# First attention head's keys, values and queries loaded after named gate tiles of the input projection

## Chip, cores and metric

One core of a Trainium2 (trn2) chip. The metric is the device time of one execution in microseconds. Times shown as a median come from three runs of the kernel; the rows come from one profiled execution of it.

## What is computed

Two layers of an encoder over 2048 tokens of width 1024. Each layer projects its normed input to 4128 columns, gives them to three branches, gates each branch with SiLU, and projects back. Cut to what matters here:

```python
h = rms_norm(x, norm_pre[layer])
proj = h @ w_in[layer]                       # 2048 x 4128
(gq, gk, gv, gg, gaf, gab, dq, dk, dv, dg, hq, hzf, hzb, hi, hg) = jnp.split(proj, offs, axis=-1)
y_a = gla_branch(...)                        # gated linear attention, a scan over chunks
y_b = diff_branch(dq, dk, dv, dg, ...)       # softmax attention, below
y_c = hgrn_branch(...)                       # gated linear recurrence, a scan over chunks
y = jnp.concatenate([y_a, y_b, y_c], axis=-1) @ w_out[layer]
x = x + rms_norm(y, norm_post[layer])

# diff_branch: 4 heads, two queries and two keys of 64 each, values of 128
q, k = rope(q, pos) * (DIFF_HD ** -0.5), rope(k, pos)
s = jnp.einsum('cbhqd,cbhkd->cbhqk', qblk, k)          # c = 0, 1
p = softmax(s);  w = p[0] - lam * p[1];  o = w @ v
o = rms_norm(o, norm_w) * (1.0 - lambda_init)
y_b = merge_heads(o) * jax.nn.silu(dg)
```

## The kernel before

**Projection.** Each fp32 matrix product is made of three: the operands are split into a high and a low part, and high by high, high by low and low by high are added in PSUM. The columns of a layer's input projection are taken in 18 blocks, mostly of 256 columns (the lists `first` and `rest`, lines 487 to 508). All 18 run for tokens 0 to 1023 (part 0) and then again for tokens 1024 to 2047 (part 1); in part 1 the split weights of a block come back from DRAM in two loads of 1 MB, whi and wlo, which POOL issues at line 226. Between the blocks of part 1 the two scans are recorded (`scans`), up to block 13. From block 14 (SC_END) on, what is left is: the second query block (`do_qk`, index 14, in which queries get their rotation), and three gate blocks (`do_gate`): 15 and 16 for attention's gate columns, 17 for the recurrence's. The pool `ak` with attention's keys (ks), values (vt) and queries (aqh, aql, the high and the low part) is opened at SC_END.

**A query tile** (`do_qk`, lines 366 to 378): 2 x 24 matmuls (L330); DVE multiplies out of PSUM into ru (L369) and rz (L371); POOL L372 adds; ACT L374 rounds to rh; POOL L375 takes the rest; SP stores rh and ru to dr_q (L377, L378), 256 KB each.

**A gate tile** (`do_gate`, 256 tokens x 256 columns, 4 tiles in a block and part): 48 matmuls (`mm_time`, L339); DVE L428 copies PSUM to z; ACT L350, L351, L352 make the softplus part lse; DVE L354 makes lsm, the log of the sigmoid; ACT L430 takes its exponential in place; POOL L432 multiplies z by the norm weights nw; POOL L433 multiplies by lsm; SP L434 stores 256 KB to dr_gate.

nw has one buffer. It is loaded by SP at L412 at the head of each block: two loads of 64 KB for blocks 15 and 16, which DVE L414 then scales, and four of 32 KB for block 17. All of ru, rz, rh, z, lse and lsm share one tag of six buffers, so a tile can't go on while the operation or store that frees its buffer has not happened.

**Attention's first operands.** `load_q(0, 0..2)` at SC_END: 3 x 8 loads of 64 KB on SP. `head_keys(0)` at SC_END + 1: four loads of 512 KB, issued by POOL for head 0 and by SP for the others. `head_values(0)` at SC_END + 2: one load of 1 MB issued by POOL. Attention's scores (L928, L929) read ks and aqh, aql; DVE L933 takes the maximum; ACT L942 the exponential. Head 1's keys have the second buffer of ks and are loaded during the gate blocks too.

**What sets the order.** The kernel is written against a tile framework that follows data dependences, inserts the semaphores, and sets each engine's order with a planner of its own before it runs. An engine executes its instructions in that order. A DMA's issue stands in the order of the engine that issues it and waits there for what it needs, so that what stands behind it waits too. A load into a tile that nobody else uses waits for the tile's memory alone.

Of the kernel before, what the change touches and what calls it, by code (L numbers as in the profile page):

```python
# [61 lines left out]
def tile_hybrid_encoder(  # L62
# [9 lines left out]
    nc = tc.nc  # L72
# [49 lines left out]
    def psum_close(key):  # L122
        psum.pop(key)[0].close()
# [168 lines left out]
    for l in range(DEPTH):  # L292
# [15 lines left out]
        with ExitStack() as s1:  # L308
# [7 lines left out]
            def acc(shape, name, part):  # L316
                turn[0] += 1
                return one_bank(shape, name, "m" if part == 0 and turn[0] % 2 else "s")

            def wload(c0, n, part, halves=False, scale=1.0):  # L320
                return w_again(wp, c0, n) if part else wload_into(wp, l, c0, n, halves, scale)
# [13 lines left out]
            def mm_rows(ps, w, t, n):  # L335
                g, cnt = t // 4, 0
                for k in range(KC):
                    for a, b in ((0, hhi), (0, hlo), (1, hhi)):
                        nc.tensor.matmul(ps, b[g][:, t % 4, k], w[a][:, k, :n], start=cnt == 0, stop=cnt == 3 * KC - 1)  # L339
                        cnt += 1  # L340

            def mm_time(w, t2, one_pool=False):
                ps = acc([P, 2, 256], "pp", 1 if one_pool else t2 // 4)
                for j in range(2):
                    mm_rows(ps[:, j], w, 2 * t2 + j, 256)
                return ps

            def log_sig(z, keep=None):
                e = ev.tile([P, 512], F32, tag="t", name="lse")
                nc.scalar.activation(e, z, AF.Abs)  # L350
                nc.scalar.activation(e, e, AF.Exp, scale=-1.0)  # L351
                nc.scalar.activation(e, e, AF.Ln, bias=one_t)  # L352
                m = ev.tile([P, 512], F32, tag="t", name="lsm")
                nc.vector.scalar_tensor_tensor(m, z, 0.0, e, op0=ALU.min, op1=ALU.subtract)  # L354
                return e, m
# [24 lines left out]
            def t2_rows(ap, t2):  # L380
                return ap[256 * t2:256 * t2 + 256, :].rearrange("(j p) c -> p j c", p=P)
# [19 lines left out]
                        nc.sync.dma_start(dr_vr[t0:t0 + 1024, i].rearrange("(c p) n -> c p n", p=P),  # L401
                                          bass.AP(odd.tensor, odd.offset + (P - 1) * 512, [(P * 512, 8), (-512, P), (1, 64)]))

            low = {}

            def do_gate(c0, d0, part):
                w = wload(c0, 288 if d0 == 0 else 256, part)
                nw = ev.tile([P, 256], F32, tag="nw", name="nw", bufs=1)
                src = {0: gla_norm, 768: hgrn_norm}.get(d0, diff_norm)
                n = src.shape[-1]  # L410
                for i in range(0, 256, n):
                    nc.sync.dma_start(nw[:, i:i + n], src[l:l + 1].to_broadcast([P, n]))  # L412
                if src is diff_norm:
                    nc.vector.tensor_scalar(nw, nw, 1.0 - lam_init, None, op0=ALU.mult)  # L414
                for t2 in range(4 * part, 4 * part + 4):
                    z = ev.tile([P, 512], F32, tag="t", name="z")
                    if d0 == 0:
                        if t2 % 2 == 0:
                            low[t2 // 2] = ev.tile([P, 4, 32], F32, tag="low", name="low", bufs=2)
                        for j in range(2):  # L420
                            t = 2 * t2 + j
                            ps = acc([P, 288], "pp", part)
                            mm_rows(ps, w, t, 288)
                            nc.vector.tensor_copy(z[:, 256 * j:256 * j + 256], ps[:, :256])
                            nc.scalar.copy(low[t2 // 2][:, t % 4], ps[:, 256:])
                    else:
                        ps = mm_time(w, t2)
                        nc.vector.tensor_copy(z, ps.rearrange("p j c -> p (j c)"))  # L428
                    _, m = log_sig(z)
                    nc.scalar.activation(m, m, AF.Exp)  # L430
                    zn = z.rearrange("p (j c) -> p j c", j=2)
                    nc.gpsimd.tensor_tensor(zn, zn, nw.unsqueeze(1).to_broadcast([P, 2, 256]), op=ALU.mult)  # L432
                    nc.gpsimd.tensor_tensor(z, z, m, op=ALU.mult)  # L433
                    nc.sync.dma_start(t2_rows(dr_gate, t2)[:, :, d0:d0 + 256], zn)  # L434

            def do_ch(c0, dst, scale, part):
                w = wload(c0, 256, part)
# [309 lines left out]

            kv, qs_of, ga_of = {}, {}, [None]

            def head_keys(h):  # L750
                k = ak.tile([P, 2, L], F32R, tag="ks", name="ks", bufs=2)
                r = slice(64 * (h % 2), 64 * (h % 2) + 64)
                for p0 in range(0, P, 32):
                    (nc.sync if h else nc.gpsimd).dma_start(
                        k[p0:p0 + 32].bitcast(F32), dr_k[h // 2, p0 // 64, p0 // 32 % 2, r].rearrange("(c p) t -> p c t", p=32))
                ks = [k[:, 0], k[:, 1]]
                kv[h] = [ks, None]

            def head_values(h):
                v = ak.tile([P, NT, P], F32, tag="vt", name="vt", bufs=2)  # L760
                nc.gpsimd.dma_start(v, dr_v[:, h * P:(h + 1) * P].rearrange("(c p) n -> p c n", p=P))
                kv[h][1] = v

# [4 lines left out]
            def load_q(h, qp):  # L768
                qh = ak.tile([P, 2, 256], F32R, tag="aqh", name="aqh", bufs=3)
                ql = ak.tile([P, 2, 256], F32R, tag="aql", name="aql", bufs=3)  # L770
                r = slice(64 * (h % 2), 64 * (h % 2) + 64)
                for i, q in enumerate((qh, ql)):
                    for p0 in range(0, P, 32):
                        nc.sync.dma_start(q[p0:p0 + 32].bitcast(F32), dr_q[h // 2, p0 // 64, i, r, qp * 256:(qp + 1) * 256]
                                          .rearrange("(c p) t -> p c t", p=32))
                qs_of[h, qp] = qh, ql
# [8 lines left out]
            for i, b in enumerate(first + rest):  # L785
                b(1)
                scans(LAG * SCHED[i] if i < SC_END else len(work))
                if i == SC_END:
                    sc_st.close()
                    psum_close("m")  # L790
                    psum_open("t", f"pst{l}", "right")
                    at_st = ExitStack()
                    ak = at_st.enter_context(tc.tile_pool(name=f"ak{l}", bufs=1, side="left"))
                    for qp in range(3):
                        load_q(0, qp)
                if i == SC_END + 1:
                    head_keys(0)
                if i == SC_END + 2:
                    head_values(0)
            w_in_st.close()  # L800
            psum_close("s")
            psum_open("b", f"psb{l}", "left")
# [387 lines left out]
```

## Time and profile before

| | |
|---|---|
| median of 3 runs | 3580.6 us (3577.68 to 3582.16) |
| the profiled execution | 3580.0 us, its span 3578.0 us |
| mean granted clock of TensorE | 0.988 of full speed |
| TensorE (PE) busy | 3491.2 us, 98% |
| TensorE's weight loads (PEld) | 3151.1 us, 88% |
| VectorE (DVE) | 2331.3 us, 65% |
| ScalarE (ACT) | 2046.3 us, 57% |
| GpSimd (POOL) | 1280.7 us, 36% |
| DMA | 544.59 MB, mean 152 GB/s |

Shares are of the span. All times in rows are microseconds from the span's start. A row of an engine's timeline ends, in brackets, with how long the engine was idle ahead of the instruction and what ended that. SPq is SP's DMA queue; a DMA in the chain of waits counts from its issue to its landing. The granted clock is given as a share of full speed: 1.00 is 2.4 GHz, 0.50 is 1.2 GHz.

### The profile page before, as it was taken

How to read it: one execution, taken by the hardware profiler on the slowest of the kernel's cores; microseconds unless marked ns; L12 is line 12 of the kernel's file. 1: busy time of each engine (PE TensorE's matmuls, PEld its weight loads, DVE VectorE, ACT ScalarE, POOL GpSimd, SP SyncE). 2: the span in 40 equal slices, each digit the busy share in tenths (PEclk: the TensorE clock that was granted, in tenths of full speed). 3: DMA queues.
4: the chain of work that ended last, by engine and by line, in shares of the span. 5: the costliest groups of instructions: out<-in, count | busy, mean ns of one | idle time of the engine just before them, and what ended most of it. 6: DMA issues, size and time to landing. Idle time of an engine off the chain costs nothing.

```text
span 3578.0 us, 62684 instructions
## 1 busy us (share of the span) xinstructions
PE 3491.2 (98%) x23296; PEld 3151.1 (88%) x23296; DVE 2331.3 (65%) x4164; ACT 2046.3 (57%) x4692; POOL 1280.7 (36%) x1302
## 2 busy tenths in 40 slices
PE   7999999999899999999999999999998999999999
PEld 7898988988889999998898999889888889999887
DVE  5333578775299988985324336777843998989733
ACT  4531457653378888874226225576524888888722
POOL 4237310013466655610032472000134765656100
PEclk9999999999999999999999999999999999999999
DMA  6667545545653353214356665555465423433143
GB/s 238 214 230 241 202 151 172 164 145 179 184 140 75 108 137 100 89 50 156 121 205 232 221 228 180 172 163 167 134 190 167 129 73 116 132 93 101 35 135 118
DMA packets 323120, 544.59 MB, mean 152 GB/s; under 512 B 49088, under 2 KB 208512, under 8 KB 304128
## 3 DMA queue, kind: packets, MB, share of 16 engines
q1 hardware_dynamic: 300032, 426.54, 37.8%
q0 software_dynamic: 20672, 111.94, 9.8%
q8 instruction: 185, 3.03, 0.4%
q10 hardware_dynamic: 2112, 2.10, 0.2%
q14 instruction: 119, 0.97, 0.1%
HBM read 313.83 MB, written 228.59 MB: 152 GB/s over the span
## 4 chain that ended last, share of the span: by engine, by line
PE 75%; DVE 13%; DMA 5%; ACT 4%; issue 1%; SPq 1%; POOL 0%; DVEq 0%; ACTq 0%; POOLq 0%
PE pp L339 15%; PE pp L330 15%; PE po L991 10%; PE pob L1100 9%; PE s L928 5%; PE s L929 5%; PE pt L980 5%; DVE mx L933 4%; PE pm L619 2%; DVE e L974 2%; PE po L692 2%; PE pu L714 1%; PE poi L875 1%; DMA dr_q<-rh 1%; DMA gt<-dr_gg 1%
## 5 line engine op out<-in xcount | busy, mean ns | idle before, releaser
L933 DVE TENSOR_REDUCE mx<-s 128x1 f32<-128x1024 f32 x512 | 623.2, 1218 | 59.5 <-PE s L929 58.0
L339 PE MATMUL pp<-whi,hhi 128*128 128x256 f32 (+1 forms) x2048 | 591.5, 289 | 19.9 <-issue 14.2
L942 ACT ACTIVATE e<-s,mx 128x1024 f32<-128x1024 f32 x512 | 572.7, 1123 | 30.1 <-DVE mx L933 12.0
L339 PE MATMUL pp<-wlo,hhi 128*128 128x256 f32 (+1 forms) x2048 | 588.9, 288 | 0.0
L339 PE MATMUL pp<-whi,hlo 128*128 128x256 f32 (+1 forms) x2048 | 587.7, 287 | 0.4 <-DVE hlo L198 0.4
L991 PEld LDWEIGHTS po<-vt,wt 128*128 128x128 f32 x4096 | 534.3, 191 | 46.0 <-ACT o L998 3.5
L991 PE MATMUL po<-vt,wt 128*128 128x128 f32 x4096 | 540.1, 275 | 1.6 <-ACT o L998 1.6
L928 PE MATMUL s<-ks,aqh 128*128 128x512 f32 x1024 | 449.8, 439 | 12.9 <-ACT e L942 11.2
L339 PEld LDWEIGHTS pp<-whi,hhi 128*128 128x128 f32 x2048 | 393.8, 192 | 23.1 <-issue 21.7
L330 PE MATMUL pp<-hhi,whi 128*128 128x512 f32 x1024 | 407.7, 398 | 0.0
L330 PE MATMUL pp<-hlo,whi 128*128 128x512 f32 x1024 | 406.7, 397 | 0.0
L330 PE MATMUL pp<-hhi,wlo 128*128 128x512 f32 x1024 | 404.5, 395 | 0.0
L929 PE MATMUL s<-ks,aql 128*128 128x512 f32 x1024 | 403.4, 394 | 0.0
L339 PEld LDWEIGHTS pp<-whi,hlo 128*128 128x128 f32 x2048 | 394.2, 193 | 1.8 <-DVE hlo L198 0.8
L339 PEld LDWEIGHTS pp<-wlo,hhi 128*128 128x128 f32 x2048 | 393.4, 192 | 1.6 <-issue 0.2
L984 ACT COPY wt<-pt 128x512 f32<-128x512 f32 x512 | 301.3, 588 | 152.3 <-PE pt L980 149.2
L974 DVE SCALAR_TENSOR_TENSOR e<-e,gam 128x1024 f32<-128x1024 f32 x256 | 350.0, 1368 | 0.0
L980 PE MATMUL pt<-ident,e 128*128 128x128 f32 x2048 | 307.8, 273 | 0.4 <-ACT wt L984 0.3
L226 POOL DMA_DIRECT2D whi<-dr_w x32 | 17.6, 550 | 667.5 <-PE pp L339 341.7
L980 PEld LDWEIGHTS pt<-ident,e 128*128 128x128 f32 x2048 | 239.9, 141 | 1.8 <-ACT wt L984 1.0
L928 PEld LDWEIGHTS s<-ks,aqh 128*128 128x128 f32 x1024 | 194.9, 190 | 42.5 <-ACT e L942 18.2
L330 PEld LDWEIGHTS pp<-hhi,whi 128*128 128x128 f32 x1024 | 192.7, 188 | 43.5 <-issue 0.2
(184 smaller groups left out, 6846.2 us busy)
## 6 DMA issues: line engine op xcount, KB each, us to landing
dr_w<-whi SPq DMA_DIRECT2D x30, 1024.0 KB, 3.9
dr_w<-wlo SPq DMA_DIRECT2D x30, 1024.0 KB, 4.9
whi<-dr_w POOLq DMA_DIRECT2D x30, 1024.0 KB, 5.5
wlo<-dr_w POOLq DMA_DIRECT2D x30, 1024.0 KB, 8.6
wraw<-in_w_in_dram POOLq DMA_DIRECT2D x56, 512.0 KB, 6.3
dr_gate<-z SPq DMA_DIRECT2D x64, 256.0 KB, 2.4
aqh<-dr_q SPq DMA_DIRECT2D x256, 64.0 KB, 2.1
aql<-dr_q SPq DMA_DIRECT2D x256, 64.0 KB, 2.1
```

The costliest lines, as they stand in the source:

```text
L330: nc.tensor.matmul(ps.rearrange("p (a t) -> p a t", t=P), w[a][:, k, c:c + P], b[g][:, :, k], start=n == 0, stop=n == 3 * KC - 1)
L339: nc.tensor.matmul(ps, b[g][:, t % 4, k], w[a][:, k, :n], start=cnt == 0, stop=cnt == 3 * KC - 1)
L619: nc.tensor.matmul(pm[hd][:, c], kc[rows, cs], qc[rows, cs], start=True, stop=True)
L928: nc.tensor.matmul(s[:, i], self.qh[:, c, js], kk, start=True, stop=False)
L929: nc.tensor.matmul(s[:, i], self.ql[:, c, js], kk, start=False, stop=True)
L933: nc.vector.tensor_reduce(mx[:, k:k + 1], self.s[k].rearrange("p a n -> p (a n)"), axis=AX.X, op=ALU.max, negate=True)
L942: nc.scalar.activation(self.es[c][:, n * 1024:(n + 1) * 1024], self.s[kk].rearrange("p a n -> p (a n)"), AF.Exp, bias=self.mx[:, m:m + 1], ...
L974: nc.vector.scalar_tensor_tensor(es[0][:, hs], es[1][:, hs], gm[:, 8 + n:9 + n], es[0][:, hs], op0=ALU.mult, op1=ALU.add)
L980: nc.tensor.transpose(pt[:, i], self.es[0][:, (4 * q + i) * P:(4 * q + i + 1) * P], ident)
L984: nc.scalar.copy(wt, self.pt[q])
L991: nc.tensor.matmul(self.po, self.wt[q][:, i], self.v[:, k], start=k == 0, stop=k == NT - 1)
L1100: nc.tensor.matmul(pos[:, n], a[:, k], b[k][:, n * 512:(n + 1) * 512], start=cnt == 0, stop=cnt == 3 * KC - 1)
```

## The change

`do_gate` leaves the last tile's lsm, as it is after L430, in `late[0]`. A new helper, `after_block(t)`, copies one column of it into tile t on DVE, and then the load of t overwrites that column. The load so waits for the copy, and the copy for the exponential of the gate tile recorded last. For head 0 alone, the keys get such a copy (recorded after block 15), the values and the first three pairs of query tiles too (recorded after block 16, to which the query loads are moved from SC_END). These are eight copies in a layer, 16 in all. Nothing else is changed; TensorE's and ACT's orders are the same as before, and from line 435 on line numbers are higher by one, from `head_keys` on by seven to eleven.

```diff
--- before.py
+++ after.py
@@ -401,7 +401,7 @@
                         nc.sync.dma_start(dr_vr[t0:t0 + 1024, i].rearrange("(c p) n -> c p n", p=P),
                                           bass.AP(odd.tensor, odd.offset + (P - 1) * 512, [(P * 512, 8), (-512, P), (1, 64)]))
 
-            low = {}
+            low, late = {}, [None]
 
             def do_gate(c0, d0, part):
                 w = wload(c0, 288 if d0 == 0 else 256, part)
@@ -432,6 +432,7 @@
                     nc.gpsimd.tensor_tensor(zn, zn, nw.unsqueeze(1).to_broadcast([P, 2, 256]), op=ALU.mult)
                     nc.gpsimd.tensor_tensor(z, z, m, op=ALU.mult)
                     nc.sync.dma_start(t2_rows(dr_gate, t2)[:, :, d0:d0 + 256], zn)
+                    late[0] = m
 
             def do_ch(c0, dst, scale, part):
                 w = wload(c0, 256, part)
@@ -747,8 +748,14 @@
 
             kv, qs_of, ga_of = {}, {}, [None]
 
+            def after_block(t):
+
+                nc.vector.tensor_copy(t, late[0][:, :1])
+
             def head_keys(h):
                 k = ak.tile([P, 2, L], F32R, tag="ks", name="ks", bufs=2)
+                if not h:
+                    after_block(k[:, 0, :1])
                 r = slice(64 * (h % 2), 64 * (h % 2) + 64)
                 for p0 in range(0, P, 32):
                     (nc.sync if h else nc.gpsimd).dma_start(
@@ -758,6 +765,8 @@
 
             def head_values(h):
                 v = ak.tile([P, NT, P], F32, tag="vt", name="vt", bufs=2)
+                if not h:
+                    after_block(v[:, 0, :1])
                 nc.gpsimd.dma_start(v, dr_v[:, h * P:(h + 1) * P].rearrange("(c p) n -> p c n", p=P))
                 kv[h][1] = v
 
@@ -770,6 +779,8 @@
                 ql = ak.tile([P, 2, 256], F32R, tag="aql", name="aql", bufs=3)
                 r = slice(64 * (h % 2), 64 * (h % 2) + 64)
                 for i, q in enumerate((qh, ql)):
+                    if not h and qp < 3:
+                        after_block(q[:, 0, :1])
                     for p0 in range(0, P, 32):
                         nc.sync.dma_start(q[p0:p0 + 32].bitcast(F32), dr_q[h // 2, p0 // 64, i, r, qp * 256:(qp + 1) * 256]
                                           .rearrange("(c p) t -> p c t", p=32))
@@ -791,12 +802,12 @@
                     psum_open("t", f"pst{l}", "right")
                     at_st = ExitStack()
                     ak = at_st.enter_context(tc.tile_pool(name=f"ak{l}", bufs=1, side="left"))
-                    for qp in range(3):
-                        load_q(0, qp)
                 if i == SC_END + 1:
                     head_keys(0)
                 if i == SC_END + 2:
                     head_values(0)
+                    for qp in range(3):
+                        load_q(0, qp)
             w_in_st.close()
             psum_close("s")
             psum_open("b", f"psb{l}", "left")
```

SP's order in layer 0 at the second query block. In the kernel before (aqh and aql are the query loads, dr_q the stores of a query tile):

```order
L733 DMA dr_u<-ut 64x3x128
L733 DMA dr_u<-ut 64x4x128
L774 DMA aqh<-dr_q 32x2x256 x4
L774 DMA aql<-dr_q 32x2x256 x3
L377 DMA dr_q<-rh 128x512
L774 DMA aql<-dr_q 32x2x256
L774 DMA aqh<-dr_q 32x2x256 x4
L774 DMA aql<-dr_q 32x2x256 x4
L774 DMA aqh<-dr_q 32x2x256 x3
L378 DMA dr_q<-ru 128x512
```

In the changed kernel, from the same two scan stores on (aga loads a piece of the gate):

```order
L734 DMA dr_u<-ut 64x3x128
L734 DMA dr_u<-ut 64x4x128
L791 DMA aga<-dr_gate 128x2x128 x3
L377 DMA dr_q<-rh 128x512
L378 DMA dr_q<-ru 128x512
L377 DMA dr_q<-rh 128x512
```

The 24 query loads no longer stand between the stores.

SP's order at the gate blocks, layer 0, in the kernel before (the dr_gate stores are those of gate blocks 15 to 17; nw are the norm weights, of block 16 and then of block 17):

```order
L434 DMA dr_gate<-z 128x2x256 x3
L412 DMA nw<-in_diff_norm_dram 128x128 x2
L434 DMA dr_gate<-z 128x2x256 x4
L412 DMA nw<-in_hgrn_norm_dram 128x64 x3
L434 DMA dr_gate<-z 128x2x256
L412 DMA nw<-in_hgrn_norm_dram 128x64
L434 DMA dr_gate<-z 128x2x256 x2
L840 DMA woraw<-in_w_out_dram 128x1024 x2
```

In the changed kernel the part up to block 16's stores (the ks here are head 1's keys):

```order
L434 DMA dr_gate<-z 128x2x256 x3
L761 DMA ks<-dr_k 32x2x2048 x2
L412 DMA nw<-in_diff_norm_dram 128x128 x2
L761 DMA ks<-dr_k 32x2x2048 x2
L434 DMA dr_gate<-z 128x2x256 x4
```

and from there to the norm weights of block 17:

```order
L785 DMA aqh<-dr_q 32x2x256 x4
L785 DMA aql<-dr_q 32x2x256 x3
L434 DMA dr_gate<-z 128x2x256
L785 DMA aql<-dr_q 32x2x256
L785 DMA aqh<-dr_q 32x2x256 x4
L785 DMA aql<-dr_q 32x2x256 x4
L785 DMA aqh<-dr_q 32x2x256 x4
L785 DMA aql<-dr_q 32x2x256 x4
L412 DMA nw<-in_hgrn_norm_dram 128x64 x4
L851 DMA woraw<-in_w_out_dram 128x1024 x2
```

Head 1's keys now stand around block 16's norm weights, and the 24 query loads ahead of block 17's.

POOL's order in layer 0 in the kernel before (whi and wlo are a block's weights, ks and vt head 0's keys and values):

```order
L226 DMA whi<-dr_w 128x2048
L226 DMA wlo<-dr_w 128x2048
L372 TENSOR_TENSOR ru<-ru,rz 128x512
L754 DMA ks<-dr_k 32x2x2048 x4
L761 DMA vt<-dr_v 128x16x128
L375 TENSOR_TENSOR ru<-ru,rh 128x512
L372 TENSOR_TENSOR ru<-ru,rz 128x512
```

In the changed kernel, from the weights of block 17 on:

```order
L226 DMA whi<-dr_w 128x2048
L226 DMA wlo<-dr_w 128x2048
L432 TENSOR_TENSOR z<-z,nw 128x512
L761 DMA ks<-dr_k 32x2x2048 x4
L433 TENSOR_TENSOR z<-z,lsm 128x512
L432 TENSOR_TENSOR z<-z,nw 128x512 x2
L433 TENSOR_TENSOR z<-z,lsm 128x512 x2
L432 TENSOR_TENSOR z<-z,nw 128x512
L433 TENSOR_TENSOR z<-z,lsm 128x512
L432 TENSOR_TENSOR z<-z,nw 128x512
L770 DMA vt<-dr_v 128x16x128
L433 TENSOR_TENSOR z<-z,lsm 128x512
```

Keys and values have moved from the query block to the gate tiles, behind block 17's weights.

DVE's order in the changed kernel, layer 0, around the new copies (L753):

```order
L753 CAST ks<-lsm 128x1
L428 COPY z<-pp 128x512
L354 SCALAR_TENSOR_TENSOR lsm<-z,lse 128x512
L428 COPY z<-pp 128x512
L354 SCALAR_TENSOR_TENSOR lsm<-z,lse 128x512
L414 TENSOR_SCALAR nw<-nw 128x256
L428 COPY z<-pp 128x512
L354 SCALAR_TENSOR_TENSOR lsm<-z,lse 128x512
...
L753 COPY vt<-lsm 128x1
L753 CAST aqh<-lsm 128x1
L753 CAST aql<-lsm 128x1
```

The keys' copy follows L354 of block 15's last tile, the others L354 of block 16's last tile; the scaling of nw (L414) stands between.

## Rows read from the trace of the kernel before

**Rows 1.** Chain of waits, layers 0 and 1: start us, us, engine, what.
```profile
888.39 20.99 DMA dr_q<-rh
...
916.51 8.24 DMA dr_q<-ru
928.35 57.84 PE pp L339 x480
...
990.65 1.20 ACT e L942 x2
...
2665.73 19.74 DMA dr_q<-rh
...
2705.51 59.32 PE pp L339 x480
...
2770.34 1.20 ACT e L942 x2
```

**Rows 2.** TensorE's timeline: start us, us, instruction [idle before <-what ended it].
```profile
912.41 0.55 PE L339 MATMUL pp<-whi,hhi 128*128 128x256 f32 x1 [7.77 <-issue]
...
928.35 0.36 PE L339 MATMUL pp<-whi,hhi 128*128 128x256 f32 x1 [2.07 <-DVE ru L369]
...
2688.51 0.55 PE L339 MATMUL pp<-whi,hhi 128*128 128x256 f32 x1 [6.38 <-issue]
...
2705.51 0.35 PE L339 MATMUL pp<-whi,hhi 128*128 128x256 f32 x1 [3.65 <-DVE ru L369]
```

**Rows 3.** Windows: us, busy PE, PEld, DVE, ACT, POOL; PEclk, DMA share, GB/s.
```profile
885.00:905.00 20.00, 19.64 (x87) 15.95 (x85) 0.69 (x1) 1.24 (x2) 7.49 (x9) 1.00 1.00 262
890.00:895.00 5.00, 5.00 (x24) 4.14 (x23) 0.00 (x0) 0.62 (x1) 2.50 (x2) 1.00 1.03 212
...
910.00:915.00 5.00, 2.58 (x12) 2.62 (x13) 1.63 (x3) 0.62 (x1) 3.88 (x5) 0.50 0.64 175
950.00:980.00 30.00, 30.00 (x252) 30.00 (x251) 9.30 (x14) 18.27 (x28) 16.59 (x14) 1.00 0.20 64
```

**Rows 4.** SP's queue: start us, us for the run of issues, what, count.
```profile
896.03 8.50 SPq L774 DMA_DIRECT2D aqh<-dr_q  x4
...
912.57 0.92 SPq L774 DMA_DIRECT2D aql<-dr_q  x2
...
954.10 0.82 SPq L412 DMA_DIRECT2D nw<-in_diff_norm_dram  x2
...
970.24 1.30 SPq L412 DMA_DIRECT2D nw<-in_hgrn_norm_dram  x3
```

**Rows 5.** POOL's timeline, columns as in rows 2.
```profile
885.29 2.18 POOL L754 DMA_DIRECT2D ks<-dr_k  x4
...
959.10 1.70 POOL L432 TENSOR_TENSOR z<-z,nw 128x512 f32<-128x512 f32 x1 [3.64 <-DVE nw L414]
960.87 1.30 POOL L433 TENSOR_TENSOR z<-z,lsm 128x512 f32<-128x512 f32 x1
...
978.57 1.29 POOL L432 TENSOR_TENSOR z<-z,nw 128x512 f32<-128x512 f32 x1 [6.98 <-DVE lsm L354]
```

**Rows 6.** DVE's timeline, columns as in rows 2.
```profile
909.56 0.69 DVE L371 TENSOR_TENSOR rz<-pp,cs 128x512 f32<-128x512 f32 x1 [20.44 <-DMA dr_q<-rh]
...
949.14 0.68 DVE L428 COPY z<-pp 128x512 f32<-128x512 f32 x1
...
952.01 0.69 DVE L354 SCALAR_TENSOR_TENSOR lsm<-z,lse 128x512 f32<-128x512 f32 x1 [2.19 <-ACT lse L352]
...
958.67 0.29 DVE L414 TENSOR_SCALAR nw<-nw 128x256 f32<-128x256 f32 x1 [1.89 <-DMA nw<-in_diff_norm_dram]
```

**Rows 7.** ACT's timeline, columns as in rows 2.
```profile
952.73 0.63 ACT L430 ACTIVATE lsm<-lsm 128x512 f32<-128x512 f32 x1 [0.76 <-DVE lsm L354]
```

**Rows 8.** The page's DMA issues: queue, count, KB each, median us to landing.
```profile
whi<-dr_w POOLq DMA_DIRECT2D x30, 1024.0 KB, 5.5
...
ks<-dr_k POOLq DMA_DIRECT2D x8, 512.0 KB, 14.2
```


## Prediction

> **What bounds the kernel now.** I read the chain of waits first, in the two stretches that the change touches, which I call L0 and L1 (the last projection blocks of layer 0 and layer 1); then TensorE's timeline there, the windows, and the timelines of SP, POOL, DVE and ACT. TensorE is busy for 98% of the span, so a change counts only by the idle TensorE time that it takes away or makes, and by a lower granted clock.
>
> In both layers the chain leaves TensorE once, at the end of the query blocks, for a store: dr_q<-rh, 20.99 us long in L0 and 19.74 in L1 [rows 1]. The DVE operation that needs its buffer waits 20.44 us for it [rows 6]. TensorE then waits 7.77 and 2.07 us in L0, 6.38 and 3.65 in L1 [rows 2]. I count from T0, the end of the last query matmul: 912.41 − 7.77 = 904.64 in L0 and 2688.51 − 6.38 = 2682.13 in L1.
>
> Why is a 256 KB store so slow? From 885 to 905 the DMA engines are full (share 1.00, 262 GB/s) [rows 3]. POOL had just issued four key loads of 512 KB [rows 5, 8], behind weights of 2 × 1024 KB [rows 8] and ahead of 1024 KB of values. On SP's queue the small query loads stand among the stores, and four of them take 8.50 us of issue where two take 0.92 later [rows 4]. The keys, values and queries wait for nothing but free memory, so they go out all at once, while attention starts 100 us later.
>
> What this costs: 480 gate matmuls in a row take 57.84 us [rows 1], 0.1205 each, so a gate tile of 48 takes 5.78 us, and the 576 of three blocks would take 69.4. They end at 928.35 + 57.84 = 986.19 in L0, T0 + 81.6, and at 2705.51 + 59.32 = 2764.83 in L1, T0 + 82.7. Lost: 12.1 and 13.3 us, part of it in the granted clock, 0.50 (1.2 GHz) in the 5 us behind the gap [rows 3]. The first exponential of attention starts at 990.65 and 2770.34 [rows 1]: **T0 + 86.0 and T0 + 88.2**. What the change is worth is how much earlier than this, after T0, that exponential starts.
>
> **What it removes.** The 24 query loads, 2 MB of keys and 1 MB of values of head 0 leave the stretch before T0, and with them the wait on the store. The store should land near the 8.24 us of its twin [rows 1] or sooner, TensorE does not stop at T0, and the gates end at T0 + 69.4. If nothing took the place of the stall, that would be 25.4 us.
>
> **What it adds, cheap.** Sixteen one-column DVE copies, eight to a layer. No such copy is in the trace; above, a 128x256 operation takes 0.29 us [rows 6], below, nothing. I take 0.2: 1.6 us a layer, beside gate work in which DVE is busy 9.3 of 30 us [rows 3]. Cost 0; uncovered, 1.6 a layer. But the copies stand in order on DVE and wait for L430 of a gate tile, as the next tile's z copy does anyway; and SP and POOL wait at the issues behind them.
>
> **What it adds, dear: the norm weights.** In the new order SP issues the norm weights of gate block 16 (nw, two loads) after the first half of head 1's keys, and at the moment when POOL issues the keys of head 0; and those of block 17 (four loads) after all 24 query loads. POOL's L432 needs nw, and six buffers are shared by all gate tiles, so when POOL stops, DVE, ACT and TensorE stop one after the other. Step by step:
>
> - The keys' copy waits for tile 4 of block 15: T0 + 4 × 5.78 + 0.68 + 2.19 + 0.69 + 0.63 [rows 6, 7] = T0 + 27.3. The four issues take 2.18 [rows 5].
> - Around T0 + 25.4 to 30 these are then asked of the DMA engines: weights 2048 KB, keys 2048 KB, half of head 1's keys 1024 KB, gate stores 256 KB, nw 128 KB: 5504 KB, 5.64 MB. At the 262 GB/s of the earlier crowd [rows 3] that is 21.5 us. So nw lands at **N ≈ T0 + 47**. Bounds: the same loads alone took 4.6 us, issued 954.10 [rows 4] and used 958.67 [rows 6]: T0 + 32.8, which binds nothing (TensorE's own pace then sets the end, as with N = T0 + 39.8). At the lowest rate, 212 GB/s [rows 3], 26.6 us: T0 + 52. I take the middle rate, because it was measured with the same keys and weights in flight.
> - From N: nw's scaling 0.29, POOL 1.70 + 3 × 1.30 [rows 5] (two tiles, since the third's buffer waits for them), DVE 0.69 and 0.68, ACT 2.19, DVE 0.69, ACT 0.63 [rows 6, 7], the copies 0.2 and some hops: the first query load is issued at N + 11.3.
> - 24 query loads and one gate store at 0.46 [rows 4] are 11.5, with 1.5 for the 1 MB of values beside them (an estimate: between 0 and the 6.6 by which four loads at 8.50 exceed four at 0.46): nw of block 17 is issued at N + 24.3.
> - It lands 8.3 later (issued 970.24 [rows 4], used 978.57 [rows 5]): N + 32.6. POOL 3 × 1.30: N + 36.5. DVE, ACT, DVE, ACT for the last tile, 4.9, and a gate store that has to land between: the last gate exponential ends, and the first of attention starts, near N + 43 = **T0 + 90**. ACT's order leaves the gate's exponential ahead of attention's.
>
> L0: 90 − 86.0 = +4.0; L1: 90 − 88.2 = +1.8. Sum **+5.8 us**. From 3580.0 (the profiled execution's time, whose span is 3578.0) it gives 3585.8; the median of the runs is 3580.6, so 3586. Each microsecond of N counts twice; N = T0 + 44 breaks even. Between N = T0 + 44 and 48 the time is 3579 to 3588. TensorE idles ahead of attention's first scores, and behind the 7.77 us gap the granted clock was 0.50 [rows 2, 3]; 5 us at half speed would cost 2.5. The chain there runs through ACT, not TensorE [rows 1], so I take 0, and 0 to 2.5 a layer as bounds.
>
> These loads, issued early, held up a store for 20.99 us [rows 1]. A rule speaks against holding them back all the same: the Trainium skill ("DMA: Bandwidth & Descriptors", Rules for kernel authors) says to issue a DMA early and to wait late; by it the present order would be the faster one. The row disagrees for the stretch before T0; for the stretch after it, no row here can.
>
> **Rivals.**
>
> *The transfers don't queue up, N ≤ T0 + 40 (faster).* One mechanism: the packets of nw share the DMA engines with the big loads from the start, instead of landing after them. For it: two norm loads landed in 4.6 us, and the share between 950 and 980 is only 0.20 [rows 3]. Against it: the query loads at 8.50 for four [rows 4], in the same company. Then TensorE's pace sets the tiles up to the query loads, the first exponential comes at T0 + 82.8 (39.8 + 43), and the sum is −3.2 − 5.4 = −8.6: 3572. Nothing lower follows, since nw of block 17 stands behind 24 query loads in any case; without that it would be T0 + 74, 26 us faster. The Trainium skill ("DMA: Bandwidth & Descriptors", Anatomy of one DMA — SWDGE (gpsimd) path) prices a DMA at about 2.0 us plus bytes over 436 GB/s; by that, as an estimate, 5.64 MB would take 13 us, N about T0 + 38, and this rival's time. The 262 GB/s of the full engines [rows 3] disagrees.
>
> *The norm weights land later, N = T0 + 48 to 52, or the query loads are slowed by the values (slower).* The place is SP's queue at gate block 16, the price 2 us of time for each of N, and it decides from N = T0 + 48 on. For it: small loads among the keys were issued at 2.1 us each, not 0.46 [rows 4]; 212 GB/s in the worst 5 us [rows 3]. Against it: fewer small loads stand in this crowd. N = T0 + 50 gives +6.0 more: 3592; T0 + 52, 3596.
>
> *It doesn't do what it says.* The stall at T0 could stay, if the weights alone slow the stores. Then everything of the after-chain shifts by 7.77 and 6.38: about 3600. Against it: the twin store, issued after the crowd, takes 8.24 us, and behind it 480 matmuls run without a gap [rows 1].
>
> **How the numbers follow.** The difference that a measurement of this kernel can tell from none is about 0.2%, 7.2 us: faster below 3573.4, slower above 3587.8. Chances: forecast, N = T0 + 44 to 48, 0.46 (same); late norm weights 0.36 and unchanged stall 0.04 (slower, 0.40); no queueing 0.14 (faster). The range reaches from the faster rival's 3572, with a microsecond of margin 3571, to N = T0 + 52 and the same, 3597; outside I leave the unchanged stall and the ends of the others.
>
> **What would show it.** Right: no TensorE gap at T0, dr_q stores landing within 8 us, gate matmuls in 69 us or so until POOL stops; L414's wait for nw ending near T0 + 47 in both layers, and POOL's L432 idle 10 us and more before; query loads issued from T0 + 58; POOL waiting again for block 17's nw until N + 33; the first exponential at T0 + 90. Wrong: nw landing within 8 us of its issue (then 3572 or less), a first exponential that follows something else than the last gate tile, a stall at T0, or a loss elsewhere, say in the scans, whose order on SP does not change, or at the first scores, if queries or values come later than I have them.

## The result, and the profile after

The changed kernel takes 3601.95 us in the median of five runs (3595.28 to 3609.07), the kernel before 3580.6; the ratio is 1.0063, with a 95% interval of 1.0043 to 1.0083. It is slower, by 15 to 30 us, where no measurable difference was forecast (3586, range 3571 to 3597). The profiled execution has a span of 3605.4 us, against 3578.0.

I read it as the forecast did: by the time from the last query matmul (T0) to the first exponential of attention. TensorE in the changed kernel; columns as in rows 2:

```profile
917.06 0.28 PE L339 MATMUL pp<-whi,hhi 128*128 128x256 f32 x1
...
986.06 0.28 PE L339 MATMUL pp<-wlo,hhi 128*128 128x256 f32 x1
...
1010.28 0.77 PE L939 MATMUL s<-ks,aqh 128*128 128x512 f32 x1 [18.91 <-DVE z L428]
...
2700.87 0.28 PE L339 MATMUL pp<-whi,hhi 128*128 128x256 f32 x1
```

The gaps of [rows 2] are gone: the first gate matmul follows the last query matmul without idle time, so T0 = 917.06 and 2700.87. The query stores that took 20.99 us [rows 1] now land in 2.1; this is the view of DMA issues for 898 to 926 (queue, count, KB each, median us to landing):

```profile
dr_q<-rh SPq DMA_DIRECT2D x6, 256.0 KB, 2.1
```

But TensorE stands still for 18.91 us at attention's start (23.34 in L1). ACT's timeline has the first exponentials (L953, behind the last gate exponential, L430):

```profile
1014.22 0.63 ACT L430 ACTIVATE lsm<-lsm 128x512 f32<-128x512 f32 x1 [1.95 <-DVE lsm L354]
1014.76 1.09 ACT L953 ACTIVATE e<-s,mx 128x1024 f32<-128x1024 f32 x1
...
2798.89 1.11 ACT L953 ACTIVATE e<-s,mx 128x1024 f32<-128x1024 f32 x1 [0.81 <-PE s L940]
```

That is T0 + 97.7 in L0 and T0 + 98.0 in L1, against 86.0 and 88.2 before [rows 1]: +11.7 and +9.8, **+21.5 us** together. The median moved by 21.4.

Where it is lost: POOL, which issues block 17's weights (L226) and 4 us later the keys, waits twice for norm weights, for block 16's and then for block 17's.

```profile
940.83 0.57 POOL L226 DMA_DIRECT2D whi<-dr_w  x1
...
945.30 2.20 POOL L761 DMA_DIRECT2D ks<-dr_k  x4
...
967.28 2.55 POOL L432 TENSOR_TENSOR z<-z,nw 128x512 f32<-128x512 f32 x2 [18.46 <-DVE nw L414]
...
1003.94 2.48 POOL L432 TENSOR_TENSOR z<-z,nw 128x512 f32<-128x512 f32 x2 [21.87 <-DMA nw<-in_hgrn_norm_dram]
```

DVE gives the first wait's end (the new copy that releases the keys, then L414 in both layers):

```profile
944.66 0.15 DVE L753 CAST ks<-lsm 128x1 fp32r<-128x1 f32 x1 [0.70 <-ACT lsm L430]
...
966.85 0.29 DVE L414 TENSOR_SCALAR nw<-nw 128x256 f32<-128x256 f32 x1 [11.41 <-DMA nw<-in_diff_norm_dram]
...
2750.22 0.29 DVE L414 TENSOR_SCALAR nw<-nw 128x256 f32<-128x256 f32 x1 [10.62 <-DMA nw<-in_diff_norm_dram]
```

SP's queue gives the second: block 16's norm weights go out within 0.1 us of POOL's keys, block 17's behind the query loads:

```profile
945.37 0.83 SPq L412 DMA_DIRECT2D nw<-in_diff_norm_dram  x2
...
979.16 2.31 SPq L785 DMA_DIRECT2D aqh<-dr_q  x4
...
984.37 4.88 SPq L785 DMA_DIRECT2D aqh<-dr_q  x4
...
994.93 1.85 SPq L412 DMA_DIRECT2D nw<-in_hgrn_norm_dram  x4
...
2762.54 1.74 SPq L785 DMA_DIRECT2D aqh<-dr_q  x4
...
2777.89 2.04 SPq L412 DMA_DIRECT2D nw<-in_hgrn_norm_dram  x4
```

The windows of the first wait, columns as in rows 3: the DMA engines are full at 218 GB/s. In the kernel before they were busy for a fifth from 950 to 980 [rows 3], when its norm weights of both blocks were loaded.

```profile
950.00:960.00 10.00, 10.00 (x85) 10.00 (x85) 1.39 (x2) 2.96 (x5) 0.00 (x0) 1.00 1.02 218
960.00:970.00 10.00, 10.00 (x86) 10.00 (x85) 0.89 (x2) 0.00 (x0) 2.72 (x3) 1.00 1.03 218
```

The second wait is another matter. While it lasts the DMA engines empty:

```profile
988.00:996.00 8.00, 2.09 (x4) 1.02 (x4) 1.92 (x2) 1.98 (x3) 0.00 (x0) 0.60 0.50 134
996.00:1002.00 6.00, 0.00 (x0) 0.00 (x0) 0.00 (x0) 0.00 (x0) 0.00 (x0) 0.50 0.08 21
```

So block 17's norm weights are late by their place in SP's order (15.8 us from the first query load to their issue), and then by their own landing, 7.3 us for a load among almost idle DMA engines (6.3 in the kernel before). No burst holds them at that point.

### The profile page after: what moved, and what is told of

Same layout as the page of the kernel before. It is cut to its first block, busy times and chain, and to the rows that moved or that the text cites. A ratio compares the mean times of both kernels' runs of the same rounds, so it can differ in the third digit from the quotient of the medians.

```text
span 3605.4 us, 62709 instructions
## 1 busy us (share of the span) xinstructions
PE 3494.7 (97%) x23296; PEld 3149.6 (87%) x23296; DVE 2332.7 (65%) x4180; ACT 2045.5 (57%) x4692; POOL 1272.2 (35%) x1302
## 5 line engine op out<-in xcount | busy, mean ns | idle before, releaser
L953 ACT ACTIVATE e<-s,mx 128x1024 f32<-128x1024 f32 x512 | 572.1, 1122 | 30.0 <-DVE mx L944 10.8
L226 POOL DMA_DIRECT2D whi<-dr_w x32 | 17.7, 553 | 671.0 <-PE pp L330 346.2
```

Of the source, the lines that this page charges most:

```text
L953: nc.scalar.activation(self.es[c][:, n * 1024:(n + 1) * 1024], self.s[kk].rearrange("p a n -> p (a n)"), AF.Exp, bias=self.mx[:, m:m + 1], ...
```

## Experiments

The first theory (A) was the forecast's: POOL waits for norm weights that land late, behind the keys and then behind the query loads. Its rival (B): the burst of loads holds up everything small, and the norm weights are only what waits first.

All were timed beside runs of the kernel before, whose median there was 3587 us; 0.001 of a ratio is 3.6 us. The table has, for L0 and L1, the first exponential after the last query matmul, from each trace as above; the sum against the kernel before's 174.2; and idle time of TensorE that came later, for the two layers. The last column is measured by itself, without the trace.

| run | L0 | L1 | against before | later gap | ratio (95%) |
|---|---|---|---|---|---|
| before | 86.0 | 88.2 | | | 1 |
| changed kernel | 97.7 | 98.0 | +21.5 | | 1.0063 (1.0043 to 1.0083) |
| the same again (e13) | 97.6 | 99.0 | +22.4 | | 1.0066 (1.0047 to 1.0085) |
| e1, norm weights early | 86.9 | 86.1 | −1.2 | | 0.9995 (0.9978 to 1.0011) |
| e2, block 17's alone | 87.2 | 87.1 | +0.1 | | 1.0013 (0.9996 to 1.0030) |
| e3, block 16's alone | 83.9 | 83.0 | −7.3 | | 0.9978 (0.9966 to 0.9990) |
| e4, before, norm weights early | 101.8 | 99.7 | +27.3 | | 1.0079 (1.0057 to 1.0102) |
| e5, head 1's keys held too | 90.4 | 90.3 | +6.5 | 35.6 | 1.0111 (1.0077 to 1.0145) |
| e7, keys alone held | 86.2 | 88.6 | +0.6 | | 1.0000 (0.9981 to 1.0020) |
| e8, queries and values alone held | 104.8 | 105.9 | +36.5 | | 1.0091 (1.0063 to 1.0119) |
| e9, spread | 73.7 | 74.8 | −25.7 | 34.8 | 1.0028 (1.0008 to 1.0047) |
| e11, spread, no later gap | 74.1 | 74.8 | −25.3 | | 0.9926 (0.9907 to 0.9944) |
| e12, e11 and norm weights early | 77.3 | 77.0 | −19.9 | | 0.9952 (0.9936 to 0.9969) |
| e14, head 0's keys earlier | 90.0 | 87.6 | +3.4 | | 1.0012 (0.9996 to 1.0028) |

The two middle columns add up to the ratio within about 5 us in every row: what these kernels differ in lies in this stretch and, for two of them, right behind it.

**e1, e2, e3: take the norm weights out of the burst.** Part 1's nw gets a tile of its own, in a pool opened at SC_END: for all three blocks (e1), for block 17 (e2), for block 16 (e3).

```diff
-                nw = ev.tile([P, 256], F32, tag="nw", name="nw", bufs=1)
+                nw = (nwp if part and d0 else ev).tile([P, 256], F32, tag=f"nw{d0}" if part and d0 else "nw", name="nw", bufs=1)
```

(e2 has `part and d0 == 768`, e3 `part and d0 == 512`.)

> The changed kernel (median 3602 us), with the gate norm weights of blocks 15, 16 and 17 of part 1 in a tile of their own each, so that their loads go out before the crowd of keys. Theory A (POOL waits for norm weights that land behind the keys, and then behind the query loads): L414 and L432 wait for nothing, the gate matmuls run through in 69 to 73 us, the first exponential comes 74 to 78 us after the last query matmul instead of 97.7, and the time is 3555 to 3562 us, 19 to 26 below the kernel before. Theory B (the crowd of loads itself holds the gates, by gate stores that land 15 us and more late or by block 17's weights; the norm weights are only what waits first): the first exponential stays at 88 us or later, 3582 us or more.

> The changed kernel, with block 17's norm weights alone in a tile of their own, loaded before the crowd; block 16's still land among the keys. Theory A: nw of block 16 lands at 49.5 us after the last query matmul as in the changed kernel, the wait of 21.9 us for block 17's is gone, first exponential at about 78, 3562 us (3558 to 3570). Theory B: POOL or DVE waits for a gate store instead, 3590 us or more.

> The changed kernel, with block 16's norm weights alone in a tile of their own; block 17's still stand behind the 24 query loads. Theory A: the first wait of 18.5 us is gone, the query loads go out 11 us earlier (51 us after the last query matmul, not 62), the second wait stays, first exponential at about 86.5, 3579 us (3574 to 3585). Theory B: 3592 us or more, with the first wait replaced by one for a gate store or for block 17's weights.

Each took 10 to 15 us a layer back. In e1 and e2 theory A had expected 74 to 78, and neither came near. e3 came out at about the time that theory A had for it (86.5 expected, 83.9 and 83.0 measured), but not by the way it named, as shown below. ACT's timeline in e1, from 965 on, shows what waits in the norm weights' place (T0 = 908.13):

```profile
965.78 0.63 ACT L350 ACTIVATE lse<-z 128x512 f32<-128x512 f32 x1 [12.61 <-DMA dr_gate<-z]
...
988.20 0.63 ACT L350 ACTIVATE lse<-z 128x512 f32<-128x512 f32 x1 [4.29 <-DMA dr_gate<-z]
...
995.07 1.11 ACT L954 ACTIVATE e<-s,mx 128x1024 f32<-128x1024 f32 x1 [3.38 <-DVE mx L948]
```

A gate store that shares the burst keeps one of the six buffers about as long as the norm weights were late, and more stores stand behind the query loads. So theory A was half of it: what holds the norm weights, the burst first and SP's order after it, holds whatever else the gate tiles need next. In e3 more changed than I had said: with block 16's tile out of the way, block 17's load also moved up, ahead of the query loads, so that it too took both waits away and ended best of the three.

**e4: the same edit in the kernel before.**

> The kernel before, with the norm weights of blocks 15 to 17 in tiles of their own. Theory A and B alike: they are not what ends the gates there (the stall at the last query tile is), so 3577 to 3585 us. A gain of 10 us and more would say that the norm weights cost the kernel before as well and that part of what the first experiments gain is not the changed kernel's loss.

It lost 27 us instead of nothing. The early norm weights went out among the query stores, in the burst that is already there, and DVE's scaling of them (L414) stands ahead of the last query tiles (L369), whose stores are then issued behind head 1's keys. SP's queue and DVE in e4:

```profile
940.72 4.18 SPq L754 DMA_DIRECT2D ks<-dr_k  x4
```

```profile
936.82 0.78 DVE L414 TENSOR_SCALAR nw<-nw 128x256 f32<-128x256 f32 x1 [11.91 <-DMA nw<-in_diff_norm_dram]
...
961.14 0.69 DVE L428 COPY z<-pp 128x512 f32<-128x512 f32 x1 [18.48 <-DMA dr_q<-rh]
```

Waits of the same kind, at another place: 11.91 for norm weights, 18.48 for a store. From here on the theory (C in the expectations) was: a burst moves at about 220 GB/s, and a small transfer issued into it lands when the burst has passed. For the changed kernel this is the first wait alone; the second lies behind the burst.

**e7, e8: one part of the change alone.** e7 takes the guards and the move from values and queries, e8 takes the guard from the keys.

```diff
# e7
-                if not h:
-                    after_block(v[:, 0, :1])
-                    if not h and qp < 3:
-                        after_block(q[:, 0, :1])
# e8
-                if not h:
-                    after_block(k[:, 0, :1])
```

> Only the keys are held back; values and queries are loaded as in the kernel before. Theory C: ahead of the last query matmul the burst is 2 MB smaller, the query store lands after some 13 us instead of 21 and TensorE's gap there is 0 to 3 us; block 16's norm weights land 49.5 us after the last query matmul as in the changed kernel; nothing stands ahead of block 17's norm weights; first exponential at 80 after the last query matmul, 83 with the gap: 10 to 16 us less than the kernel before, ratio 0.996 to 0.997. If the queries' place is of no account, the first exponential stays at 97 and the ratio at 1.006.

> Only the values and queries are held back; the keys of head 0 are loaded as in the kernel before, and head 1's keys go out with them, ahead of the second query block's stores. Theory C: the burst before the last query matmul is as large as in the kernel before (2 MB weights, 2 + 2 MB keys), the query store takes 20 us and more and TensorE's gap stays, 7 to 12 us; block 16's norm weights then land in time; the 24 query loads still stand ahead of block 17's, first exponential 92 to 100 us after the last query matmul: 10 to 24 us more than the kernel before, ratio 1.003 to 1.007. If the queries on SP's queue made the stall of the kernel before, the gap is gone and the ratio is 0.998 or less.

e7 kept the time of the kernel before, 13 us short of what I expected. The gap at T0 is gone, but with queries and values still ahead of T0 a query store is late (10.59 us below; without them, in the changed kernel, these stores landed in 2.1), so the gate tiles start late, the norm weights are issued later, and land at T0 + 54.0 (970.21 − 916.21) instead of 49.8. DVE in e7:

```profile
927.70 0.69 DVE L369 TENSOR_TENSOR ru<-pp,cs 128x512 f32<-128x512 f32 x1 [10.59 <-DMA dr_q<-ru]
...
970.21 0.29 DVE L414 TENSOR_SCALAR nw<-nw 128x256 f32<-128x256 f32 x1 [14.75 <-DMA nw<-in_diff_norm_dram]
```

e8 is slower still than I expected: with head 0's keys early, head 1's went out early as well, the store took longer, and TensorE's gap at T0 doubled. DVE and TensorE in e8:

```profile
929.55 0.69 DVE L369 TENSOR_TENSOR ru<-pp,cs 128x512 f32<-128x512 f32 x1 [24.46 <-DMA dr_q<-rh]
```

```profile
930.34 0.55 PE L339 MATMUL pp<-whi,hhi 128*128 128x256 f32 x1 [15.17 <-issue]
```

So the stall of the kernel before comes with the keys: without them (e7) TensorE has no gap at T0, though a query store is still late; without the query loads and the values there (e8) the gap stays. That it is larger there may come from head 1's keys, which moved up as well; this was not tried apart.

**e5, e14: make the burst at block 16's norm weights smaller.** e5 holds head 1's keys too; e14 releases head 0's keys at the first gate tile of block 15 instead of the last.

```diff
# e5
-                if not h:
+                if h < 2:
                     after_block(k[:, 0, :1])
# e14: called in do_gate behind that tile
+                    hooks[256, 4] = [lambda: head_keys(0)]
-                    head_keys(0)
```

> The changed kernel, with head 1's keys held as well, until the last gate tile of block 17. That takes 1 MB out of the loads ahead of block 16's norm weights and changes nothing else in the chain. Theory C (a burst of loads moves at about 220 GB/s, and every small transfer issued into it, norm weights or gate store, lands when the burst has passed): the norm weights land 4.8 us earlier, 45 us after the last query matmul, the first exponential at 93 instead of 98, 9 to 10 us less in the two layers: 3592 us, ratio to the kernel before about 1.003. If head 1's keys don't count, the time stays at the changed kernel's, ratio 1.006.

> The changed kernel with one moment other: head 0's keys wait for the first gate tile of block 15, not its last, so that they no longer go out with block 17's weights. Head 1's keys then move up on SP's queue, ahead of block 15's stores. Theory C: block 16's norm weights meet 2 MB instead of 5.5 and land in time (their scaling 40 us or less after the last query matmul, no wait of POOL over 10 us there), the 24 query loads go out at 51 instead of 62 and still stand ahead of block 17's norm weights: first exponential at 86 to 89, 18 to 24 us less than the changed kernel in the two layers, ratio 0.999 to 1.001. If the queries' place alone made the loss, it stays at 97 and the ratio at 1.006.

e14 came within 2 us of what was expected (40 for L414, 86 to 89 for the first exponential): POOL's first wait is down to 4 us, the second, behind the query loads, has not changed. So each of the two waits can be taken away without the other: e14 leaves the second alone and gains 7.7 and 10.4 us a layer, e2 leaves the first alone and gains 10.5 and 10.9. DVE and POOL in e14 (T0 = 913.88, so L414 at T0 + 41.7):

```profile
955.56 0.29 DVE L414 TENSOR_SCALAR nw<-nw 128x256 f32<-128x256 f32 x1 [0.48 <-DMA nw<-in_diff_norm_dram]
```

```profile
955.99 1.31 POOL L432 TENSOR_TENSOR z<-z,nw 128x512 f32<-128x512 f32 x1 [4.38 <-DVE nw L414]
...
993.10 2.48 POOL L432 TENSOR_TENSOR z<-z,nw 128x512 f32<-128x512 f32 x2 [21.80 <-DMA nw<-in_hgrn_norm_dram]
```

In e5 the stretch became shorter, by more than expected (90 instead of 98, with 93 forecast), but the time did not: TensorE stands still for 18.19 and 17.43 us, from some 42 us after the first exponential on. The next runs show where that comes from.

**e9, e11, e12: spread the loads.** e9 releases the keys of head 0 at the first gate tile of block 15, the queries at the second of block 16, the values at its last, and the keys of head 1 at the last tile of all. In e9, as in e5, the copy that holds head 1's keys is recorded within attention, where `head_load(1)` stands. e11 records it, and the loads, right behind the last gate tile, and lets POOL issue them. e12 adds the norm weights of e1.

```diff
# e9, called in do_gate behind the tile named; head_keys(1) guarded as in e5
+                    hooks[256, 4] = [lambda: head_keys(0)]
+                    hooks[512, 5] = [lambda qp=qp: load_q(0, qp) for qp in range(3)]
+                    hooks[512, 7] = [lambda: head_values(0)]
# e11
+                    hooks[768, 7] = [lambda: head_keys(1)]
-                    (nc.sync if h else nc.gpsimd).dma_start(
+                    (nc.sync if h > 1 else nc.gpsimd).dma_start(
-                head_keys(h)
+                if h > 1:
+                    head_keys(h)
```

> The changed kernel with other moments: head 0's keys after the first gate tile of block 15, the three query pairs after the second tile of block 16, the values after its last, head 1's keys after the last gate tile of all; norm weights as in the changed kernel. Theory C: no burst is larger than 2 MB (weights and keys follow each other), so no store or norm weight waits long enough to stop TensorE; gap at the last query matmul 0, gates 69 to 70 us, first exponential at 74 to 78: 20 to 27 us less than the kernel before in the two layers, ratio 0.993 to 0.995. If something that the bursts have hidden ends the stretch (gate stores behind the query loads, the scores), the first exponential is at 84 or later and the ratio 0.998 or more.

> The run with the spread loads, but head 1's keys are issued by POOL right after the last gate tile, when its trace had the DMA engines idle, instead of by SP 30 us later, beside the loads of the scans' states (ust). Theory C: first exponential again 74 to 75 us after the last query matmul in both layers, and the 17 us of idle TensorE that the run with the spread loads had 40 us after that is gone: 26 us less than the kernel before, ratio 0.992 to 0.994. If that later gap came from something else than head 1's keys beside the states, it stays and the ratio is 1.00 or more.

> The same with the norm weights of blocks 15 to 17 in tiles of their own, loaded before the bursts. POOL's 10 us wait for block 17's norm weights goes, but TensorE does not wait there any more: ratio within 0.002 of the run without it. A gain of 0.003 or more would say that the norm weights still cost something with spread loads; a loss of as much, that their early loads among the query stores cost something, as in the kernel before with norm weights of their own.

In e9 the stretch is as short as the forecast's floor (74 us, which is 69.4 of gate matmuls and the last tile's way to ACT), and 17.42 us are given back behind it. TensorE and ACT in e9, then POOL, DVE and SP's queue:

```profile
1041.26 2.08 PE L1001 MATMUL po<-vt,wt 128*128 128x128 f32 x8 [17.42 <-ACT o L1008]
```

```profile
1040.94 0.27 ACT L1008 COPY o<-po 128x128 f32<-128x128 f32 x1 [18.32 <-POOL aga L1018]
```

```profile
1012.08 0.52 POOL L820 MEMSET ust<- 64x512 f32 x1 [28.06 <-DVE mx L956]
...
1026.39 1.62 POOL L835 TENSOR_TENSOR st<-ust,tst 64x512 f32<-64x512 f32 x1 [13.24 <-DMA ust<-dr_u]
```

```profile
1011.74 0.14 DVE L755 CAST ks<-lsm 128x1 fp32r<-128x1 f32 x1
```

```profile
1013.15 1.14 SPq L824 DMA_DIRECT2D ust<-dr_u  x2
1014.34 2.31 SPq L763 DMA_DIRECT2D ks<-dr_k  x4
```

Read upwards: SP loads the scans' states (ust), POOL waits for them, POOL's output gating (L1018) stands behind that in order, ACT waits for it, and TensorE for ACT. My reading before e11 was that head 1's held keys, which go out beside the states, make them late. The rows don't bear that out: POOL waits about as long for the states where no keys stand beside them, as in the kernel before, and longer in e11, which has no later gap. POOL in the kernel before and in e11:

```profile
995.42 0.52 POOL L810 MEMSET ust<- 64x512 f32 x1 [2.64 <-PE s L929]
...
1008.27 1.45 POOL L825 TENSOR_TENSOR st<-ust,tst 64x512 f32<-64x512 f32 x1 [11.76 <-DMA ust<-dr_u]
```

```profile
991.15 2.19 POOL L763 DMA_DIRECT2D ks<-dr_k  x4
993.97 0.52 POOL L822 MEMSET ust<- 64x512 f32 x1 [0.63 <-DMA dr_gate<-z]
...
1013.67 1.05 POOL L837 TENSOR_TENSOR st<-ust,tst 64x512 f32<-64x512 f32 x1 [18.63 <-DMA ust<-dr_u]
```

What differs is when the states' loads start: 5 us after the first exponential in the kernel before and in e11, 31 us after it in e9 and e5. POOL clears a part of ust first, and in e9 that waits 28.06 us, until the copy that holds head 1's keys has run on DVE (at 1011.74; in e5 the copy is at 1030.00 and the clearing at 1030.34). The copy reads lsm. By the code, ust lies in memory that the pool of lsm and z leaves free, and in e11 the clearing waits for a gate store of z (the row above); so I take it that the late copy kept that memory occupied. e11 changed the copy's place, the keys' moment and their issuer at once; which of these removed the gap was not tried apart. TensorE (T0) and ACT in e11:

```profile
914.95 0.28 PE L339 MATMUL pp<-whi,hhi 128*128 128x256 f32 x1
```

```profile
989.08 1.10 ACT L954 ACTIVATE e<-s,mx 128x1024 f32<-128x1024 f32 x1
...
2756.36 1.10 ACT L954 ACTIVATE e<-s,mx 128x1024 f32<-128x1024 f32 x1
```

e11 beats both kernels: 3560.5 us beside 3586.8, by about the 25.4 us that the prediction named for the case that nothing takes the stall's place. e12 (0.9952) lost 2 to 3 us a layer against it, a little more than expected, though the two intervals touch: in its order on DVE the copy that holds head 1's keys stands ahead of the first maximum. That is read from the order; it was not tried apart.

**e13: the changed kernel again.**

> The changed kernel unchanged, beside the same runs of the kernel before: first exponential at 97 to 98 us after the last query matmul in both layers, some 21 us more than the kernel before in the two, no loss after that: ratio 1.005 to 1.008. If the two layers' stretch is as long as before but the ratio is not, the difference lies in the scans' part.

The loss is the same, and nearly all of it is in the two stretches: 22.4 us, where the ratio makes 24.

## Why the prediction was wrong

**What it removes: right.** No gap at T0, stores at 2.1 us, gate matmuls in 69.3 us (917.06 to 986.34).

**What it adds, cheap: right.** The copies take 0.14 to 0.15 us, and in the changed kernel nothing but the loads that they hold waits for them.

**What it adds, dear: the right chain, every term too small. This is the step that failed.** The five steps stood in the order forecast, at the places forecast, and each took longer than the sum had it. What they measured, in L0 and L1:

| step | forecast | L0 | L1 |
|---|---|---|---|
| N, block 16's norm weights used, after T0 | 47 | 49.8 | 49.4 |
| N to the first query load | 11.3 | 12.3 | 12.3 |
| query loads and one store, to block 17's norm weights | 13.0 | 15.8 | 15.4 |
| their landing | 8.3 | 9.0 | 9.3 |
| from there to the first exponential | 10.4 | 10.8 | 11.7 |
| first exponential after T0 | 90 | 97.7 | 98.0 |

Each miss is 0.4 to 2.8 us, none of them large, but they stand in a row on one chain that is run through twice: 7.7 and 8.0 us a layer, 15.7 in all, which is the whole difference between +5.8 and +21.5. Two of them, N and the query loads, make two thirds of it. N was taken at 262 GB/s [rows 3]; the 5.64 MB took the 26.0 us from the weights' issue (940.83, T0 + 23.8 where T0 + 25.4 was forecast) to the use of nw (966.85), which is 217 GB/s, close to the 212 that I had kept as a bound. And the query loads beside the values: 1.5 us was allowed, out of bounds of 0 to 6.6; four of them took 4.88 where four took 1.74 to 2.31 just ahead of the values. The landing, 8.3, was read from a row whose wait DVE's lsm had ended [rows 5], not the norm weights, so it was no measured landing; from issue to use it took 9.0 and 9.3.

**The rival "later norm weights": right, and priced too low.** N lay in its 48 to 52, and its second half, queries slowed by the values, came true at the same time. Its price had N alone. The bounds of the other terms were in the text and never reached the range: N = T0 + 50 alone gave 3592, and 2 or 3 us more on the query loads, twice, make 3596 to 3598, before the landing and the last tile add anything. The 0.46 for "no change" rested on the middle value of every term at once.

**"The transfers don't queue up": wrong.** The norm weights were issued at 945.37 and used at 966.85, 21.5 us later, though they are 128 KB. The estimate worked out from the Trainium skill ("DMA: Bandwidth & Descriptors", Anatomy of one DMA — SWDGE (gpsimd) path), 13 us for the whole burst (15 with the 2.0 us of the same formula, which the estimate left out), is little more than half of the 26.0 that it took; the measurement decides.

**What the prediction did not see.** It said that with norm weights that don't queue up, and without block 17's behind the query loads, the time would be 26 us less. e1, in which POOL waits for neither, shows that it would not: the gate stores are next, in the same burst and behind the same query loads. And it took the norm weights for the cause of the first wait where the cause is the burst, 5.6 MB released within 7 us: by the weights' own need and by the copies at the same tile. For the second wait its cause holds, the place behind 24 query loads on SP. With the loads of both heads spread over the gate tiles by copies of the same kind, the change is worth 26 us (e11).

**What stays open.** Whether the late copy alone made the later gap of e5 and e9, as the rows suggest, was not tried apart. Which share of e3's lead over e1 (4 to 6 us) comes from the place of head 1's keys and which from the stores was not tried apart.

## What to carry to other kernels

Holding a load back moves its burst; it does not remove it. Before choosing the moment, list what else is issued around it (here 5.64 MB at the measured 217 GB/s held the norm weights up until 26 us after the burst began), what stands behind the load in the order of the engine that issues it, and which shared buffers hang on those small transfers. A release spread over the gate tiles, in pieces of 1 to 2 MB, turned a loss of 22 us into a gain of 26. Record the copy that holds a load near the tile that it reads: recorded late, it may keep that tile's memory occupied. And when a sum has five terms in one chain, carry their bounds into the range together.

## What the runs showed of the hardware

A burst moved at 217 GB/s with the DMA engines full, and engines waited some 20 us for small transfers in it: DVE 20.44 for a 256 KB store beside POOL's keys [rows 6], 24.46 for one with POOL's and SP's keys together (e8); norm weights of 128 KB were used 21.5 us after their issue. Without a burst such a store landed in 2.1 us. The norm weights of block 17, 32 KB a load, took 6.3 us from issue to landing in the kernel before and 7.3 in the changed one, while the DMA engines were busy for 0.15 and then less than 0.1 of the time.

The Trainium skill ("DMA: Bandwidth & Descriptors", Rules for kernel authors) says that loads issued by SP, ACT and GpSimd run on the same 16 DMA engines and interleave, and that spreading them over issuers only saves issue time. These waits on SP's stores behind POOL's loads agree; no run here changes the issuer alone.

The part before T0, in which TensorE's order is the same, moved by more than the forecast's 0.2%. T0 of layer 0 lies at 904.6 in the profile of before, 917.1 after, and 904.0 when the changed kernel was run again. The granted clock goes with it: in the stretch from 500 to 600 it was 0.93 of full speed (2.4 GHz for part of the time, 1.2 for the rest) in the first profile of the changed kernel and 1.00 when run again. The same window, of after and of e13:

```profile
500.00:600.00 100.00, 97.29 (x579) 83.22 (x578) 76.22 (x144) 64.72 (x149) 3.22 (x6) 0.93 0.53 168
```

```profile
500.00:600.00 100.00, 97.68 (x615) 83.67 (x614) 78.04 (x146) 68.52 (x156) 3.23 (x6) 1.00 0.54 171
```

So a time read from a single profile can be off by some 10 us here; the stretch that the change touches is the better measure.
